# First two stripes side by side on the raw input, a third and layer 1's second one in float32, layer norm's additions on VectorE, two heads kept in SBUF

## The chip, the cores and the metric

The kernel runs on one core of one Trainium2 chip. A core has a matrix engine (TensorE, PE in the profile), a vector engine (VectorE, DVE), an activation engine (ScalarE, ACT), a general engine (GpSimd, POOL) and queues that start DMA transfers (SP is SyncE, whose only work here is to start them). The engines run their own instruction lists in order and wait for each other by semaphores. The metric is the device time of one execution in microseconds (us), the median over runs.

## The reference

Two residual layers over 528 rows (16 meta tokens and 512 inputs) of width 2048, and a final norm. Cut to what matters:

```python
def even_mixer(hn, ...):                       # layer 0
    glu_v, glu_g, gate_a, q, c, gate_b, qi, ki, wi = split_last(hn @ w_in, EVEN_SPLITS)
    u = causal_depthwise_conv(glu_v * sigmoid(glu_g), width=31) + conv_b
    a_out = silu(layer_norm(u, ln_g, ln_b)) * silu(gate_a)
    c = rms_norm(c, kv_g)                      # 256 columns, the shared keys and values
    ...                                        # index scores from qi, ki, wi pick 128 keys a query
    b_out = (attention of 8 heads over the picked keys) * silu(gate_b)
    return concatenate([a_out, b_out]) @ w_out
def odd_mixer(hn, ...):                        # layer 1
    q, fz, i, g = split_last(hn @ w_in, 4 x 2048)
    ...                                        # gated linear recurrence, 16 heads, chunks of 64
    return (rms_norm per head of the recurrence * silu(g)) @ w_out
for layer in range(2):
    h = h + mixer(rms_norm(h, norm_gain[layer]))
return rms_norm(h, final_norm_gain)[:, 16:]
```

## The kernel before, in words

Everything is kept transposed: 128 features on the partitions, the 528 rows (T) along the free axis, usually as two halves of 264 (HT). A width of 2048 is 16 tiles (KT). The weights arrive as stripes: w[s] is 128 x 2048 in float32, 1 MB, all that is needed for 128 outputs. `load_raw` brings one into a ring of three buffers (`w32`; `w` in the profile).

There are two ways to multiply a stripe. `stripe` works on a normalised input that has been split into two float16 parts (X0 in layer 0, X1 in layer 1; tiles `x` and `mx`). ACT sums the stripe's squares (L192, `junk`), POOL adds them over the partitions (`all_sum`, L144, an all-reduce), VectorE makes a power-of-two scale of it (L148 to L201), ACT and VectorE split the weights into `wh` (L208) and `wl` (L209), in two halves each and rings of five; then PE does three float16 products for each of the 16 tiles and each column half, 96 matmuls (L251 to L253). A stripe with `wide=False` leaves the meta rows out and has 48 matmuls of 512 columns. `raw_stripe` works on the input as it is, in float32: VectorE multiplies the norm's gain into the weights (L264), PE does one float32 product for each tile and half (L267; the trace shows two passes for each), and the evacuation multiplies by the row's reciprocal norm (`evac`, L279). It needs neither X nor rstd to begin.

At the start, 16 x tiles (names z, Kh, Vt, mb, from the rings that are free then) and the first weights come through SP's queue in the order of the code. ACT squares each x tile (L377, L380), VectorE adds the squares in three groups (L381), PE sums them over the partitions with a matrix of ones (`mean_bcast`, L304, `ones_d`), ACT makes rstd0 of it by a logarithm and an exponential (`rstd_from`, L311 and L312), and VectorE and ACT make X0 from it (L388, then `split`: L293 on ACT, L294 on VectorE). kw (80 columns: index keys and index weights) is a raw stripe on these tiles; its evacuation is followed by four small transposes on PE (L409). The two stripes of c are c0, a raw stripe, and c1, an ordinary one.

Then come eight gated convolutions (`glu`), 64 scores and selections, the layer norm and eight heads, in a hand-written order of steps. `layer_norm` sums the eight convolved tiles Z, takes the mean from Z[i] (L675) and sums the squares: ACT squares (L680), POOL adds (L681, tile `acc`), and PE takes the mean square (L304 with `ones_a`). Each head leaves its output tile `mb` in DRAM (`mbd`, L647). Before the output projection all eight are read back (L732), scaled by a factor that depends on all of layer 0's statistics and split into `mx` (the last one into an `x`).

Layer 1 begins with fz of head 0, a raw stripe on the residual sum h, then the mean and rstd1, X1 (L793 and `split`), and q and v of head 0 as ordinary stripes. For each of 16 heads three stripes (fz, q, v) go through PE, and `rec_head` does the recurrence of that head beside them. On POOL's queue `send` prepares sums of later weights in DRAM, one or two steps after each ordinary stripe.

The program order on each engine is set by a scheduler that simulates the program when it is built and takes, among ready instructions, those of the highest priority band: WGT (weights, X), EVAC (evacuations, norms), SIDE (attention, gates, recurrence), CONV (convolution, layer norm). `queued[...]` and `behind(...)` (`issue_after`) hold an instruction back until another one has been placed. So a change of one part can move instructions elsewhere.

Of the kernel before, what the change touches and what calls it, by code (L numbers as in the profile page):

```python
# [74 lines left out]
def trunk_kernel(ctx: ExitStack, tc: tile.TileContext, x: bass.AP, w: bass.AP, wukv: bass.AP,  # L75
# [5 lines left out]
    def band(level):  # L81
        return tc.high_priority(level * 1000000)
# [149 lines left out]
    def columns(wide):  # L232
        return (slice(0, HT), slice(HT, T)) if wide else (slice(NM, T),)
# [19 lines left out]
                    P.matmul(o, lo[half][:, ws], xh[:, sl], start=False, stop=n == 1 and k == 7)  # L253
        return parts, inv

    def raw_stripe(w32, X, gain, m=128, ring=None):

        ring = [r or bank for r in ring or (None, None)]
        parts = [(r(), sl) for r, sl in zip(ring, columns(True))]
        parts = [(p[:, :sl.stop - sl.start], sl) for p, sl in parts]  # L260
        with band(WGT):
            for n in range(2):
                v = w32[:, 1024 * n:1024 * (n + 1)].rearrange("p (k m) -> p k m", m=128)[:, :, :m]
                V.tensor_tensor(v, v, vec[:, gain + 8 * n:gain + 8 * n + 8, None].to_broadcast([128, 8, m]), op=OP.mult)  # L264
        for k in range(KT):
            for o, sl in parts:
                P.matmul(o[:m], w32[:, k * 128:k * 128 + m], X[k][:, sl], start=k == 0, stop=k == KT - 1)  # L267
        return parts

    def put(dst, parts, inv):  # L270

# [4 lines left out]
    def evac(dst, parts, rstd):  # L276
        o = T - dst.shape[-1]
        for p, sl in parts:
            V.tensor_tensor(dst[:, sl.start - o:sl.stop - o], p[:dst.shape[0]], rstd[:dst.shape[0], sl],  # L279
                            op=OP.mult)  # L280
# [27 lines left out]
    def rstd_from(pieces, dst, eps, tmp=None):  # L308

        for p, sl in pieces:  # L310
            S.activation(dst[:, sl], p, AF.Ln, bias=eps)  # L311
            S.activation(dst[:, sl], dst[:, sl], AF.Exp, scale=-0.5)  # L312
            if tmp is not None:
                t = tmp[:, sl]
                S.activation(t, dst[:, sl], AF.Square)
                V.scalar_tensor_tensor(t, p, eps, t, op0=OP.add, op1=OP.mult)
                S.activation(t, t, AF.Identity, scale=-0.5, bias=c15)
                V.tensor_tensor(dst[:, sl], dst[:, sl], t, op=OP.mult)


    bdram = dram.tile([HB, 16, BL], F32, name="bdram")
# [33 lines left out]

    X0 = []
    xin = []
    with band(WGT + 1):
        for k in range(KT):
            shape, name, bufs = STAGE[k]  # L360
            hin = et(shape, F32, name, bufs)
            if len(shape) > 2:
                hin = hin.rearrange("p a b -> p (a b)")
            hin = hin[:, :T]
            Q.dma_start(hin, x[k])
            if k == 0:
                wkw = load_raw(S_KW, 2)
            if k == 11:
                wc = load_raw(S_C)
            xin.append(hin)  # L370
    sums = []
    with band(EVAC):
# [8 lines left out]
                V.tensor_tensor(acc0, acc0, sq, op=OP.add)  # L381
    rstd0 = et([128, T], F32, "rstd", 1)
    with band(EVAC):
        rstd_from(mean_bcast(ones_d, sums, None, ring=(pso, ps1)), rstd0, eps_r)
    with band(WGT):
        for k in range(KT):
            t = et([128, T], F32, "sq", 3)
# [11 lines left out]


    kw = et([128, T], F32, "qh", 2)
    ps = raw_stripe(wkw, xin, V_G0, m=80)
    with band(EVAC):
        evac(kw[:80], ps, rstd0)
    wiT = et([128, NB, NM], F32, "wiT", 1)
    with band(SIDE):
        p = ps1()
        for t in range(NB):
            P.transpose(p[:, t * NM:(t + 1) * NM], kw[64:80, NM + 128 * t:NM + 128 * (t + 1)],  # L409
                        ident[64:80, 64:80])  # L410
        V.tensor_scalar(wiT.rearrange("p a b -> p (a b)"), p[:, :NB * NM], 1.0 / 32, None, op0=OP.mult)

        ki = et([128, T], F32, "gt", 3)
        G.dma_start(ki[:64], kw[:64])
        G.dma_start(ki[64:], kw[:64])


        kih = epools["ei"].tile([128, T], F32R, name="kih", bufs=1)
        kil = epools["ei"].tile([128, T], F32R, name="kil", bufs=1)
        S.activation(kih, ki, AF.Identity)  # L420
        V.tensor_tensor(kil[:64], ki[:64], kih[:64].bitcast(F32), op=OP.subtract)
        V.tensor_tensor(kil[64:], ki[64:], ki[64:], op=OP.subtract)
# [6 lines left out]
    csq = []  # L429
    for j in range(2):  # L430
        c = et([128, T], F32, "gb", 2)
        if j == 0:
            ps = raw_stripe(wc, xin, V_G0, ring=(ps1, ps1))
            with band(EVAC):
                evac(c, ps, rstd0)
        else:
            ps, inv = stripe(S_C + j, X0, back0, ring=(None, ps1))
            with band(EVAC):
                put(c, ps, inv)
        with band(SIDE):  # L440
            sq = et([128, T], F32, "sq", 3)
            S.activation(sq, c, AF.Square)
        cn.append(c)
        csq.append(sq)
# [152 lines left out]
    def attend(h, qh, gb, Kh, Vt):  # L597
# [46 lines left out]
        p = ps1()  # L644
        P.matmul(p[:, :NM], Vt[:NM, 0, :], pt[:NM, 0, :NM], start=True, stop=True)
        V.tensor_tensor(mb[:, :NM], p[:, :NM], gb[:, :NM], op=OP.mult)
        Q.dma_start(mbd[h], mb)  # L647

    def head(h):
        if h % 2 == 0:  # L650
# [13 lines left out]
    def layer_norm():  # L664
        with band(CONV):
            zs = et([128, T], F32, "acc", 2)
            V.tensor_tensor(zs, Z[0], Z[1], op=OP.add)
            for i in range(2, 8):
                V.tensor_tensor(zs, zs, Z[i], op=OP.add)
            mu = et([128, T], F32, "acc", 2)  # L670
            for p, sl in mean_bcast(ones_a, [zs], None):
                S.activation(mu[:, sl], p, AF.Copy)
            vs_ = et([128, T], F32, "acc", 2)
            for i in range(8):
                V.tensor_tensor(Z[i], Z[i], mu, op=OP.subtract)  # L675
                if i == 0:
                    S.activation(vs_, Z[i], AF.Square)
                else:
                    sq = et([128, T], F32, "sq", 3)
                    S.activation(sq, Z[i], AF.Square)  # L680
                    G.tensor_tensor(vs_, vs_, sq, op=OP.add)  # L681
            rz = et([128, T], F32, "acc", 2)
            rstd_from(mean_bcast(ones_a, [vs_], None), rz, eps_l)
        return rz
# [26 lines left out]
    with band(SIDE):  # L711
# [13 lines left out]
        V.tensor_scalar(c[6], mscale, 0.25, None, op0=OP.mult)  # L725
        V.tensor_scalar(c[7], mscale, 0.5, None, op0=OP.mult)
        for i in range(8):
            shape, name = (([128, T], "Kh"), ([128, 5, 128], "Vt"), ([128, T], "L"))[i // 3]
            mb = et(shape, F32, name, 3)
            if len(shape) > 2:  # L730
                mb = mb.rearrange("p a b -> p (a b)")[:, :T]
            Q.dma_start(mb, mbd[i])  # L732
            MX[8 + i] = split(r1p.tile([128, 2, T], F16, name="mx" if i < 7 else "x", bufs=7 if i < 7 else KT), mb, c[7])
        for i in range(8):
            MX[i] = split(r1p.tile([128, 2, T], F16, name="x", bufs=KT), MA[i], c[6])
# [44 lines left out]
                V.tensor_tensor(acc1, acc1, sq, op=OP.add)  # L780
            S.dma_start(h1d[n], hin)
    with band(WGT):
        wfz = load_raw(S_FQV)
    ps0 = raw_stripe(wfz, H1, V_G1)
    with band(EVAC):
        with tc.issue_after(done.ins):
            S.preload_act_table_set("natural_log_exp_and_others")
# [198 lines left out]
    for h in range(16):  # L986
# [2 lines left out]
        v = ht([128, T], F32, "v", 2)  # L989
        if h == 0:  # L990
            with band(EVAC):
                evac(fz, ps0, rstd1)
        for dst, i in ((fz, 0), (q, 1), (v, 2)):
            if h or i:
                ps, inv = stripe(S_FQV + 3 * h + i, X1, back1, wide=i != 1)
                with band(EVAC):
                    put(dst, ps, inv)
                send(todo, 1 + i % 2)
# [328 lines left out]
```

## Time and profile before

| | before |
|---|---|
| median of 3 runs | 1872.37 us (1872.37, 1875.14, 1872.37) |
| the profiled execution | 1873.82 us, span 1872.0 us, mean granted PE clock 0.986 |
| PE busy | 1815.4 us, 97% |
| VectorE busy | 1339.1 us, 72% |
| ACT busy | 1203.5 us, 64% |
| POOL busy | 194.7 us, 10% |
| DMA | 272.79 MB, mean 146 GB/s |

A timeline row reads: start in us, busy us of the group, engine, line, operation, output tile <- input tiles, shape, and xN for the number of instructions in the group; in brackets the idle time of that engine just before, and what ended it. A row of waits reads: who waited, the tile and line it waited to work on, <- whose result on which tile and line; then us in total, how often, and the longest. A windows row gives, after the stretch and its length, the busy time of PE, PE's weight loads, DVE, ACT and POOL, then the granted PE clock, the share of the DMA engines that was busy, and GB/s. Lines are those of the kernel before.

### The profile page before, as it was taken

How to read it: one execution, taken by the hardware profiler on the slowest of the kernel's cores; microseconds unless marked ns; L12 is line 12 of the kernel's file. 1: busy time of each engine (PE TensorE's matmuls, PEld its weight loads, DVE VectorE, ACT ScalarE, POOL GpSimd, SP SyncE). 2: the span in 40 equal slices, each digit the busy share in tenths (PEclk: the TensorE clock that was granted, in tenths of full speed). 3: DMA queues.
4: the chain of work that ended last, by engine and by line, in shares of the span. 5: the costliest groups of instructions: out<-in, count | busy, mean ns of one | idle time of the engine just before them, and what ended most of it. 6: DMA issues, size and time to landing. Idle time of an engine off the chain costs nothing.

```text
span 1872.0 us, 36780 instructions
## 1 busy us (share of the span) xinstructions
PE 1815.4 (97%) x14934; PEld 1405.2 (75%) x14934; DVE 1339.1 (72%) x2758; ACT 1203.5 (64%) x1941; POOL 194.7 (10%) x353
## 2 busy tenths in 40 slices
PE   8999999899999599999999999999999999999997
PEld 5777578788888577888677777777777775446886
DVE  7699999997565255444586777777777776666775
ACT  6655665466555565444578887788877877765562
POOL 1100100121211222000111001010110000001000
PEclk9999999999999799999999999999999999999999
DMA  6432333234344145333465554554545345656553
GB/s 246 112 102 96 96 112 103 83 114 126 104 140 127 37 132 182 136 122 137 143 182 161 168 169 140 177 170 159 169 142 152 122 151 179 207 197 229 202 190 112
DMA packets 65434, 272.79 MB, mean 146 GB/s; under 512 B 8272, under 2 KB 15736, under 8 KB 48144
## 3 DMA queue, kind: packets, MB, share of 16 engines
q1 hardware_dynamic: 36128, 180.36, 27.1%
q0 software_dynamic: 17616, 52.19, 11.7%
q10 hardware_dynamic: 11520, 37.88, 6.0%
q8 instruction: 117, 1.92, 0.4%
q14 instruction: 53, 0.43, 0.1%
HBM read 251.30 MB, written 40.58 MB: 156 GB/s over the span
## 4 chain that ended last, share of the span: by engine, by line
PE 89%; DVE 4%; DMA 3%; ACT 2%; issue 2%; POOL 1%; SPq 0%; DVEq 0%; POOLq 0%; ACTq 0%
PE mps L252 23%; PE mps L251 23%; PE mps L253 23%; PE mps L1145 8%; PE po L635 1%; PE s L610 1%; DVE mask L556 1%; PE s L267 1%; DVE m L555 1%; PE s L846 1%; PE s L845 1%; PE s L847 1%; PE po L968 1%; PE po L967 1%; DMA w<-in_w_dram 1%
## 5 line engine op out<-in xcount | busy, mean ns | idle before, releaser
L251 PE MATMUL mps<-x,wh 128*128 128x264 f16 (+1 forms) x3216 | 955.8, 297 | 5.4 <-ACT x L293 2.2
L252 PE MATMUL mps<-x,wh 128*128 128x264 f16 (+1 forms) x3216 | 956.0, 297 | 1.7 <-DVE x L294 1.7
L253 PE MATMUL mps<-x,wl 128*128 128x264 f16 (+1 forms) x3216 | 955.7, 297 | 0.0
L252 PEld LDWEIGHTS <-wh 128*128 128x128 f16 x3456 | 339.0, 98 | 128.0 <-issue 16.2
L253 PEld LDWEIGHTS <-wl 128*128 128x128 f16 x3456 | 339.0, 98 | 117.2 <-issue 5.5
L251 PEld LDWEIGHTS <-wh 128*128 128x128 f16 x3456 | 338.9, 98 | 116.8 <-issue 4.1
L208 ACT ACTIVATE wh<-w,sc 128x1024 f16<-128x1024 f32 x224 | 256.0, 1145 | 260.3 <-PE mps L252 225.1
L209 DVE SCALAR_TENSOR_TENSOR wl<-w,sc,wh 128x1024 f16<-128x1024 f32 x224 | 287.4, 1284 | 141.3 <-ACT wh L208 140.8
L192 ACT ACTIVATE junk<-w 128x2048 bf16<-128x2048 f32 (+1 forms) x116 | 214.7, 1851 | 3.7 <-DMA w<-in_w_dram 3.1
L581 DVE SCALAR_TENSOR_TENSOR z<-u,vec,z 128x528 f32<-128x528 f32 x240 | 181.0, 761 | 2.3
L144 POOL PARTITION_ALL_REDUCE tot<-ss x96 | 43.6, 454 | 893.2 <-ACT junk L192 827.2
L1145 PEld LDWEIGHTS <-wh 128*128 128x128 f16 x912 | 89.2, 98 | 10.9 <-issue 0.3
L208 ACT ACTIVATE wh<-w,oq 128x1024 f16<-128x1024 f32 x53 | 60.7, 1148 | 54.6 <-PE mps L1145 46.3
L209 DVE SCALAR_TENSOR_TENSOR wl<-w,oq,wh 128x1024 f16<-128x1024 f32 x53 | 67.8, 1283 | 27.9 <-ACT wh L208 27.7
L1145 PE MATMUL mps<-on,wh 128*128 128x256 f16 x464 | 78.1, 273 | 0.1
L192 ACT ACTIVATE junk<-gw 128x1024 bf16<-128x1024 f32 x64 | 67.3, 1052 | 2.1 <-DMA gw<-in_w_dram 0.8
L251 PE MATMUL mps<-mx,wh 128*128 128x264 f16 x224 | 62.3, 278 | 3.8 <-ACT gt L274 3.8
L842 DVE SCALAR_TENSOR_TENSOR qlm<-q,qhm 128x256 f16<-128x256 f32 x128 | 52.5, 420 | 17.0 <-ACT qhm L841 16.9
L1145 PE MATMUL mps<-on,wl 128*128 128x256 f16 x232 | 63.2, 273 | 0.0
L841 ACT ACTIVATE qhm<-q 128x256 f16<-128x256 f32 x128 | 51.4, 415 | 18.4 <-DVE q L943 18.3
L253 PE MATMUL mps<-mx,wl 128*128 128x264 f16 x224 | 62.4, 279 | 0.0
L252 PE MATMUL mps<-mx,wh 128*128 128x264 f16 x224 | 62.4, 279 | 0.0
(437 smaller groups left out, 2844.1 us busy)
## 6 DMA issues: line engine op xcount, KB each, us to landing
w<-in_w_dram SPq DMA_DIRECT2D x132, 1024.0 KB, 4.9
gw<-in_w_dram ACTq DMA_DIRECT2D x64, 512.0 KB, 7.0
os<-in_w_dram POOLq DMA_DIRECT2D x42, 512.0 KB, 8.3
w<-os SPq DMA_DIRECT2D x28, 512.0 KB, 4.4
w<-in_w_dram SPq DMA_DIRECT2D x23, 512.0 KB, 4.6
os<-os POOLq DMA_DIRECT2D x14, 512.0 KB, 6.1
h<-in_x_dram POOLq DMA_DIRECT2D x16, 264.0 KB, 6.7
h1d<-h ACTq DMA_DIRECT2D x16, 264.0 KB, 2.2
```

The lines of the kernel that those rows point to most:

```text
L144: queued["G"] = G.partition_all_reduce(out, src, channels=128, reduce_op=op or bass_isa.ReduceOp.add)
L192: S.activation(junk[:, :src.shape[-1]], src, AF.Square, accum_out=ss)
L208: queued["S"] = S.activation(hi, src, AF.Identity, scale=sc)
L209: V.scalar_tensor_tensor(lo, src, sc, hi, op0=OP.mult, op1=OP.subtract)
L251: P.matmul(o, hi[half][:, ws], xh[:, sl], start=n == 0 and k == 0, stop=False)
L252: P.matmul(o, hi[half][:, ws], xl[:, sl], start=False, stop=False)
L253: P.matmul(o, lo[half][:, ws], xh[:, sl], start=False, stop=n == 1 and k == 7)
L267: P.matmul(o[:m], w32[:, k * 128:k * 128 + m], X[k][:, sl], start=k == 0, stop=k == KT - 1)
L581: eng.scalar_tensor_tensor(z, u[:, j:j + T], col(V_CW + i * CW + j), z, op0=OP.mult, op1=OP.add)
L841: S.activation(hi, src, AF.Copy, scale=scale)
L842: V.scalar_tensor_tensor(lo, src, scale, hi, op0=OP.mult, op1=OP.subtract)
L1145: P.matmul(p, wt[:, sl], xt, start=start and k == i == 0, stop=stop and k == 7 and i == 2, skip_group_check=stop and not start and resume)
```

## The change

Five edits:

- `raw_stripes` takes the place of `raw_stripe`: it takes several stripes and goes through the 16 tiles once, doing each tile for all of them. kw and c0 go through it together; c1 follows as a raw stripe of its own. c0's weight is loaded behind the fourth x tile (it was the twelfth), c1's behind the eleventh.
- The four transposes behind kw are held back until the last raw matmul of these has been placed, and the weights' square sums until rstd0's last instruction.
- The layer norm's seven additions of squares go from POOL to VectorE.
- Heads 6 and 7 of layer 0 keep their tile `mb` in SBUF; six heads go through DRAM. The six are read into the rings Kh and Vt in turn, and L is not used.
- In layer 1 v of head 0 is a raw stripe behind fz, with its weight loaded beside fz's. It has no `send` of its own.

```diff
-    def raw_stripe(w32, X, gain, m=128, ring=None):
+    def raw_stripes(X, gain, todo):
...
+        jobs = []
+        for w32, m, ring in todo:
...
         for k in range(KT):
-            for o, sl in parts:
-                P.matmul(o[:m], w32[:, k * 128:k * 128 + m], X[k][:, sl], start=k == 0, stop=k == KT - 1)
-        return parts
+            for w32, m, parts in jobs:
+                for o, sl in parts:
+                    queued["P"] = P.matmul(o[:m], w32[:, k * 128:k * 128 + m], X[k][:, sl],
+                                           start=k == 0, stop=k == KT - 1)
+        return [parts for w32, m, parts in jobs]
...
-            if k == 11:
-                wc = load_raw(S_C)
+            if k in (3, 10):
+                wc.append(load_raw(S_C + k // 10))
...
-        rstd_from(mean_bcast(ones_d, sums, None, ring=(pso, ps1)), rstd0, eps_r)
+        queued["S"] = rstd_from(mean_bcast(ones_d, sums, None, ring=(pso, ps1)), rstd0, eps_r)
...
-    ps = raw_stripe(wkw, xin, V_G0, m=80)
+    ps, cps = raw_stripes(xin, V_G0, [(wkw, 80, (None, None)), (wc[0], 128, (ps1, ps1))])
+    cps = [cps] + raw_stripes(xin, V_G0, [(wc[1], 128, (None, ps1))])
...
-        for t in range(NB):
+        with behind("P"):
+          for t in range(NB):
             P.transpose(p[:, t * NM:(t + 1) * NM], kw[64:80, NM + 128 * t:NM + 128 * (t + 1)],
...
-        if j == 0:
-            ps = raw_stripe(wc, xin, V_G0, ring=(ps1, ps1))
-            with band(EVAC):
-                evac(c, ps, rstd0)
-        else:
-            ps, inv = stripe(S_C + j, X0, back0, ring=(None, ps1))
-            with band(EVAC):
-                put(c, ps, inv)
+        with band(EVAC):
+            evac(c, cps[j], rstd0)
...
-        Q.dma_start(mbd[h], mb)
+        if h < 6:
+            Q.dma_start(mbd[h], mb)
+        else:
+            MB.append(mb)
...
-                    G.tensor_tensor(vs_, vs_, sq, op=OP.add)
+                    V.tensor_tensor(vs_, vs_, sq, op=OP.add)
...
-            shape, name = (([128, T], "Kh"), ([128, 5, 128], "Vt"), ([128, T], "L"))[i // 3]
-            mb = et(shape, F32, name, 3)
+            shape, name = (([128, T], "Kh"), ([128, 5, 128], "Vt"))[i % 2]
+            mb = MB[i - 6] if i >= 6 else et(shape, F32, name, 3)
...
-            Q.dma_start(mb, mbd[i])
+            if i < 6:
+                Q.dma_start(mb, mbd[i])
...
-        wfz = load_raw(S_FQV)
-    ps0 = raw_stripe(wfz, H1, V_G1)
+        wfz, wv = load_raw(S_FQV), load_raw(S_FQV + 2)
+    ps0 = raw_stripes(H1, V_G1, [(wfz, 128, (None, None))])
+    ps0 += raw_stripes(H1, V_G1, [(wv, 128, (ps1, ps1))])
...
-                evac(fz, ps0, rstd1)
+                evac(fz, ps0[0], rstd1)
+                evac(v, ps0[1], rstd1)
         for dst, i in ((fz, 0), (q, 1), (v, 2)):
-            if h or i:
+            if h or i == 1:
```

What it moves, in the order of the instructions. Lines of the kernel after are a few higher: L267 is L271 there, L304 is L309, L602 and L604 are L605 and L607. First PE at the start: the x tiles are z (the first eight), Kh, Vt and mb; `w_203` is kw's weight in both, `w_228` before and `w_212` after that of c0; `po` and `s_288` (`s_290` after) are the two halves of the mean. Before:

```order
L267 MATMUL mps<-z,w_203 80x264 x14
L304 MATMUL po<-acc,ones_d 128x264
L304 MATMUL s_288<-acc,ones_d 128x264
L267 MATMUL mps<-z,w_203 80x264 x2
L267 MATMUL mps<-Kh,w_203 80x264 x5
L304 MATMUL po<-acc,ones_d 128x264
L304 MATMUL s_288<-acc,ones_d 128x264
L267 MATMUL mps<-Kh,w_203 80x264
L267 MATMUL mps<-Vt,w_203 80x264 x6
L267 MATMUL mps<-mb,w_203 80x264 x4
L304 MATMUL po<-L,ones_d 128x264
L304 MATMUL s_288<-L,ones_d 128x264
```

After, around the last pair of ones:

```order
L271 MATMUL mps<-Kh,w_203 80x264 x2
L271 MATMUL s_383<-Kh,w_212 128x264
L271 MATMUL s_384<-Kh,w_212 128x264
L309 MATMUL po<-L,ones_d 128x264
L309 MATMUL s_290<-L,ones_d 128x264
L271 MATMUL mps<-Kh,w_203 80x264 x2
L271 MATMUL s_383<-Kh,w_212 128x264
L271 MATMUL s_384<-Kh,w_212 128x264
L271 MATMUL mps<-Vt,w_203 80x264 x2
L271 MATMUL s_383<-Vt,w_212 128x264
L271 MATMUL s_384<-Vt,w_212 128x264
```

Before, the last pair of ones stands behind all 32 matmuls of kw; now behind 20 of kw and 20 of c0, with nine tiles of kw ahead of c0's first row and the two stripes in turn from the tenth tile on.

POOL around the layer norm; `stat<-ss` is an all-reduce of a stripe's squares, a row of `ISA` without tiles stands where POOL turns to another kind of operation, the DMAs are those of the heads' bias rows. Before:

```order
L144 ISA stat<-ss 128x1
L681 ISA
L681 TENSOR_TENSOR acc<-acc,sq 128x528 x6
L144 ISA
L144 ISA stat<-ss 128x1
L681 ISA
L681 TENSOR_TENSOR acc<-acc,sq 128x528
L144 ISA
L144 ISA stat<-ss 128x1
```

After:

```order
L605 DMA L<-bdram 128x1x400
L607 DMA L<-mask_580 128x400
L144 ISA stat<-ss 128x1 x3
L605 DMA L<-bdram 128x1x528
L607 DMA L<-mask_583 128x528
L144 ISA stat<-ss 128x1
```

The seven additions have left, and the turns with them.

PE at the start of layer 1; the tiles h are the residual sums, `w_10655` is fz's weight before, `w_10568` after, `w_10570` that of v, and the rows with `ones_d` are the mean. Before:

```order
L267 MATMUL mps<-h_9262,w_10655 128x264 x2
L267 MATMUL mps<-h_9389,w_10655 128x264
L304 MATMUL s_10694<-acc_8621,ones_d 128x264
L304 MATMUL s_10696<-acc_8621,ones_d 128x264
L267 MATMUL mps<-h_9389,w_10655 128x264
L267 MATMUL mps<-h_9516,w_10655 128x264 x2
```

After:

```order
L271 MATMUL mps<-h_10191,w_10568 128x264 x2
L271 MATMUL s_10608<-h_8538,w_10570 128x264
L271 MATMUL s_10609<-h_8538,w_10570 128x264
L309 MATMUL s_10645<-acc_8534,ones_d 128x264
L309 MATMUL s_10647<-acc_8534,ones_d 128x264
L271 MATMUL s_10608<-h_8540,w_10570 128x264
L271 MATMUL s_10609<-h_8540,w_10570 128x264
```

The mean stood behind 17 of fz's 32 matmuls; it stands behind all 32 and the first pair of v, and 15 pairs of v follow it ahead of q.

More of the change, by code (lines that the diff above doesn't have):

```diff
@@ L254, in stripe @@
         return parts, inv
-    def raw_stripe(w32, X, gain, m=128, ring=None):
[L258 to L264, printed above, removed]
-        for k in range(KT):
-            for o, sl in parts:
-                P.matmul(o[:m], w32[:, k * 128:k * 128 + m], X[k][:, sl], start=k == 0, stop=k == KT - 1)
-        return parts
+    def raw_stripes(X, gain, todo):
+        jobs = []
+        for w32, m, ring in todo:
+            ring = [r or bank for r in ring]
+            parts = [(r(), sl) for r, sl in zip(ring, columns(True))]
+            jobs.append((w32, m, [(p[:, :sl.stop - sl.start], sl) for p, sl in parts]))
+            with band(WGT):
+                for n in range(2):
+                    v = w32[:, 1024 * n:1024 * (n + 1)].rearrange("p (k m) -> p k m", m=128)[:, :, :m]
+                    V.tensor_tensor(v, v, vec[:, gain + 8 * n:gain + 8 * n + 8, None].to_broadcast([128, 8, m]),
+                                    op=OP.mult)
+        for k in range(KT):
+            for w32, m, parts in jobs:
[3 more added lines that the diff above has]
+        return [parts for w32, m, parts in jobs]
     def put(dst, parts, inv):
@@ L311, in rstd_from @@
             S.activation(dst[:, sl], p, AF.Ln, bias=eps)
-            S.activation(dst[:, sl], dst[:, sl], AF.Exp, scale=-0.5)
+            done = S.activation(dst[:, sl], dst[:, sl], AF.Exp, scale=-0.5)
             if tmp is not None:
@@ L318, in rstd_from @@
                 V.tensor_tensor(dst[:, sl], dst[:, sl], t, op=OP.mult)
+        return done
     bdram = dram.tile([HB, 16, BL], F32, name="bdram")
@@ L357, in trunk_kernel @@
     xin = []
+    wc = []
     with band(WGT + 1):
@@ L727, in trunk_kernel @@
         for i in range(8):
-            shape, name = (([128, T], "Kh"), ([128, 5, 128], "Vt"), ([128, T], "L"))[i // 3]
-            mb = et(shape, F32, name, 3)
-            if len(shape) > 2:
+            shape, name = (([128, T], "Kh"), ([128, 5, 128], "Vt"))[i % 2]
+            mb = MB[i - 6] if i >= 6 else et(shape, F32, name, 3)
+            if len(mb.shape) > 2:
                 mb = mb.rearrange("p a b -> p (a b)")[:, :T]
-            Q.dma_start(mb, mbd[i])
+            if i < 6:
+                Q.dma_start(mb, mbd[i])
             MX[8 + i] = split(r1p.tile([128, 2, T], F16, name="mx" if i < 7 else "x", bufs=7 if i < 7 else KT), mb, c[7])
```

## Prediction

> **What bounds the kernel now.** I read the page's first table and its chain first, then PE's waits over the whole span, then the timelines of PE, ACT, DVE, POOL and SP around the four places that the change touches.
>
> ```profile
> span 1872.0 us, 36780 instructions
> PE 1815.4 (97%) x14934; PEld 1405.2 (75%) x14934; DVE 1339.1 (72%) x2758; ACT 1203.5 (64%) x1941; POOL 194.7 (10%) x353
> PE 89%; DVE 4%; DMA 3%; ACT 2%; issue 2%; POOL 1%; SPq 0%; DVEq 0%; POOLq 0%; ACTq 0%
> ```
>
> PE is busy 1815.4 of 1872.0 us and carries 89% of the chain that ended last. So time can leave in two ways only: PE waits less (56.6 us in all), or PE has less to do, which includes running less at half clock. The list of PE's waits says where those 56.6 us lie:
>
> ```profile
> PE s L304 <- POOL acc L681: 20.0, 1, 20.0
> PE s L409 <- DVE qh L279: 5.2, 1, 5.2
> PE mps L251 <- ACT gt L274: 5.1, 3, 3.8
> ```
>
> In order: the layer norm's mean square, the wait before the four small transposes at the start, and the start of layer 0's output projection. The change touches these three and a fourth place, layer 1's first stripes, where the waits are short and many (part 4). I price one after the other.
>
> **1. Layer norm: seven additions go from POOL to VectorE.**
>
> ```profile
> 609.49 9.07 POOL L681 TENSOR_TENSOR acc<-acc,sq 128x528 f32<-128x528 f32 x6 [9.99 <-issue]
> 626.13 0.40 POOL L144 PARTITION_ALL_REDUCE stat<-ss  x1 [7.57 <-issue]
> 633.71 1.28 POOL L681 TENSOR_TENSOR acc<-acc,sq 128x528 f32<-128x528 f32 x1 [7.18 <-issue]
> 600.54 5.03 DVE L675 TENSOR_TENSOR z<-z,acc 128x528 f32<-128x528 f32 x8
> 605.49 1.27 DVE L209 SCALAR_TENSOR_TENSOR wl<-w,sc,wh 128x1024 f16<-128x1024 f32 x1
> 602.46 1.15 ACT L208 ACTIVATE wh<-w,sc 128x1024 f16<-128x1024 f32 x1
> 610.82 0.64 ACT L680 ACTIVATE sq<-z 128x528 f32<-128x528 f32 x1 [5.78 <-POOL acc L681]
> 615.18 1.90 ACT L192 ACTIVATE junk<-w 128x2048 bf16<-128x2048 f32 x1
> 635.05 2.13 PE L304 MATMUL s<-acc,ones_a 128*128 128x264 f32 x4 [20.04 <-POOL acc L681]
> 619.00:638.00 19.00, 2.95 (x9) 2.54 (x10) 1.71 (x4) 3.68 (x5) 1.69 (x2) 0.50 0.16 64
> ```
>
> POOL stands 9.99, 7.57 and 7.18 us ("issue": nothing that the trace shows) each time it turns from a reduction to an addition or back, and an addition there takes 1.3 us or more. The seventh addition lies behind both turns, so PE stands 20.04 us, until 635.05. With the additions on VectorE the three reductions follow each other without a turn. VectorE's addition: 5.03/8 = 0.63 us. It has 8 subtractions (5.03), one L209 (1.27) and 7 additions (4.4) from 600.54 on, so it could be done at 611.2. ACT sets the pace: its row order stays, with one weight split and the 1.90 us junk square ahead of the last square. The split before stood at 602.46; they come when PE frees a buffer, some 6 to 7 us apart there, so this one at 609.3; the junk ends at 612.3 with its 0.2 us read, the square at 612.9, the last addition at 613.6. PE's arrival was 635.05 - 20.04 = 615.0, and it now has a few more matmuls first. So the wait goes entirely, with 1.4 us to spare. Behind the idleness PE ran at half clock: the last row (a stretch, then PE's busy time, and after POOL's the granted clock) has 2.95 busy us at 0.50, of which half, 1.5, is lost. Term: 20.0 + 1.5 = 21.5. Next to come late is the split for the stripe behind; its all-reduce no longer waits 7.57 us, so I take nothing. Bounds: 22 above; below 11.5, if ACT's and VectorE's chain comes a stripe's length (10 us) late.
>
> **2. Heads 6 and 7 kept in SBUF.**
>
> ```profile
> 721.94 0.33 SPq L732 DMA_DIRECT2D L<-mbd  x1
> 728.14 0.74 ACT L293 ACTIVATE x<-L,mxb 128x528 f16<-128x528 f32 x1 [7.54 <-DMA L<-mbd]
> 736.09 0.46 ACT L274 ACTIVATE gt<-mps,inv 128x264 f32<-128x264 f32 x1
> 738.00:741.00 3.00, 3.00 (x16) 2.03 (x15) 2.00 (x3) 0.86 (x2) 0.00 (x0) 0.50 0.40 167
> ```
>
> ACT stood 7.54 us for head 7's tile to return from DRAM. Everything behind on ACT moved with it, up to the evacuation at 736.09 that gave PE its bank: PE waited 3.8 us (the longest of the three in the list) and then ran 3.00 us at half clock, 1.5 lost. Without the loads ACT comes up to 7.5 us sooner, more than the 3.8 that PE waited. Term 3.8 + 1.5 = 5.3; bounds 3 (ACT then waits for another operand) and 6. SP loses two stores and two loads, and nothing queues there.
>
> **3. The start: kw and c0 advance together, c1 also in float32.**
>
> ```profile
> 9.36 6.50 PE L267 MATMUL mps<-z,w 128*80 128x264 f32 x28
> 31.77 0.28 PE L409 MATMUL s<-ident,qh 16*128 16x16 f32 x1 [5.22 <-DVE qh L279]
> 31.98 9.02 PE L267 MATMUL s<-z,w 128*128 128x264 f32 x26
> 49.77 0.28 PE L251 MATMUL mps<-x,wh 128*128 128x264 f16 x1
> 916.03 6.84 PE L267 MATMUL mps<-h,w 128*128 128x264 f32 x30
> 32.00:33.00 1.00, 1.00 (x3) 0.82 (x3) 1.00 (x3) 1.00 (x3) 0.12 (x1) 0.50 0.44 115
> 30.17 0.72 ACT L312 ACTIVATE rstd<-rstd 128x264 f32<-128x264 f32 x2
> 10.28 3.49 ACT L380 ACTIVATE sq<-z 128x528 f32<-128x528 f32 x5 [4.24 <-DMA z<-in_x_dram]
> 10.00:12.50 2.50, 2.50 (x12) 1.55 (x11) 1.81 (x3) 1.98 (x4) 0.00 (x0) 1.00 1.05 396
> 59.63 0.72 ACT L293 ACTIVATE x<-sq,gains 128x528 f16<-128x528 f32 x1
> ```
>
> From layer 1's raw stripe (the row at 916.03; the next stripe begins at 922.71, part 4) a pass of 264 float32 columns takes 6.68/30 = 0.2227 us, so a raw stripe of 64 passes 14.25. An f16 stripe of 96 matmuls takes 10.80 (v in part 4, 940.85 to 951.65). Before, f16 work begins at 49.77, and c1's share of it ends the part that the change replaces at 49.77 + 10.80 = 60.57. After, PE does three raw stripes (192 passes) and 12 passes of ones: 204 x 0.2227 = 45.4. From 9.36 that ends at 54.8 if PE never stands.
>
> It does stand: at 396 to 400 GB/s a 1 MB weight takes 2.6 us and an x tile 0.69. c0's weight now goes behind the fourth x tile instead of the twelfth, so the fifth tile lands 2.6 later: ACT begins on the second at 10.28, so the fifth was there at 10.28 + 3 x 0.69 = 12.35, and is now at 14.95. PE has done four k's of kw by then (each 4 passes, 0.89) at 12.95. So 2.0 us of idleness, and 0.4 for the transposes: 57.2. Term 60.57 - 57.2 = 3.4. c1's 14.25 against 10.8 is in it. What hides the rest: the gain folds of c0 and c1 on VectorE fall between the x additions, before PE asks for either stripe, and a fold that comes late makes PE wait for it; the evacuations move beside the f16 stripe.
>
> Who is late next: the mean (last ones at about 31 instead of 25.9), and with it rstd0, which gains table loads on ACT too, and X0. X0's last split stood within two or three us of 60 with rstd0 ready at 30.17 + 0.72 = 30.9; some 6 us later it is 66, and the first f16 stripe asks for its sixteenth tile at 57.2 + 15 x 0.675 = 67.3 (six matmuls of 0.1125 a tile). That is tight. Bounds: above 5.4, if PE doesn't stand at 12.95; below -2, if X0 comes some 5 us late.
>
> Whether the 2.0 us of idleness halve the clock decides 1.5 more. Before, the clock fell behind 3.8 us (part 2) and behind 5.22 (0.50 in the row at 32 us). It also fell behind the 2.24 of part 4, though shorter pieces of idleness stood ahead of that one. I take no fall, since 2.0 stands alone and below all three; with it the term would be 1.9. The Trainium skill ("TensorE: Matmul & The Clock Gate", Part 1, the table of states) has the clock fall after one idle window of about 3.4 us. By that the term stays 3.4 here; but the 2.24 us of part 4 was followed by half clock, which that rule alone doesn't give.
>
> **4. Layer 1: the first v stripe in float32, after fz.**
>
> ```profile
> 915.79 0.93 ACT L311 ACTIVATE rstd<-s,eps_r 128x264 f32<-128x264 f32 x2 [5.14 <-PE s L304]
> 917.37 1.95 DVE L793 TENSOR_TENSOR sq<-h,rstd 128x528 f32<-128x528 f32 x3 [6.62 <-ACT rstd L312]
> 922.71 0.38 PE L251 MATMUL mps<-x,wh 128*128 128x512 f16 x1
> 926.59 0.38 PE L251 MATMUL mps<-x,wh 128*128 128x512 f16 x1
> 932.64 0.58 PE L251 MATMUL mps<-x,wh 128*128 128x512 f16 x1 [2.24 <-ACT x L293]
> 934.00:936.00 2.00, 2.00 (x6) 0.69 (x5) 2.00 (x4) 0.73 (x1) 2.00 (x3) 0.50 0.98 383
> 938.72 1.65 DVE L294 SCALAR_TENSOR_TENSOR x<-sq,gains,x 128x528 f16<-128x528 f32 x2
> 940.85 0.27 PE L251 MATMUL mps<-x,wh 128*128 128x264 f16 x1
> 951.65 0.28 PE L251 MATMUL mps<-x,wh 128*128 128x264 f16 x1
> 952.00:1492.00 540.00, 540.00 (x5154) 418.97 (x5152) 418.51 (x1000) 429.35 (x721) 50.27 (x103) 1.00 0.51 158
> ```
>
> The q stripe (48 matmuls; the first 18 took 926.59 - 922.71 = 3.88, so 10.35 in all) ran from 922.71 to 940.85: 18.14 us, 7.8 lost to X1 coming tile by tile and to the half clock that followed. v then ended at 951.65. After, raw v occupies PE from 922.7 to 936.9, and q could end at 947.3: a gain of 4.4 at most. But the order puts the mean behind all of fz and one pair of v: it ends at 922.7 + 0.9 = 923.6, where it was 916.0 (the next fz passes began at 916.03). VectorE started 1.3 us behind the mean and took from 917.37 to 938.72 + 1.6, 22.9 us, for X1. So now 924.9 to 947.8; q's last matmuls follow, 948.6. Term 951.65 - 948.6 = 3.1; bounds 4.4 and -2, if rstd1 comes 5 us later still behind the weight work that ACT now does first.
>
> In the 15 heads behind, the order shifts the recurrence about one stripe later. I cost that at nothing: PE stood nowhere from 952 to 1492 (540.00 of 540.00), while DVE and ACT were busy 78% and 80%, so each has a fifth of a stripe's time, 2 us, to catch up in.
>
> **The sum**: 21.5 + 5.3 + 3.4 + 3.1 = 33.3 us. The profiled execution took 1873.8 with its span of 1872.0, so 1840.5 against it; it stands 1.45 above the median of 1872.37, against which I predict 1839.1. All terms at their upper ends give 37.8 (1834.6), all at the lower 10.5 (1861.9). What this measurement can tell from no change is 0.2%, 3.7 us.
>
> **The rivals.**
>
> Late layer norm (0.10). The last square on ACT stands behind the weight split at 609, which waits for PE to free a buffer, and that is the only cover: if it slips a stripe, 10 us of wait and the cold clock return. Term 11.5 instead of 21.5, so 1849. Against it: VectorE and ACT both had several us without work there (5.78 on ACT's row at 610.82, for POOL alone).
>
> Nothing from the two ends (0.16). X0 and X1 come late, and PE's waits only move: terms 3 and 4 are -2 each instead of 6.5 together, so 1849.6. For it: both rest on a mean that comes 5 to 7 us later than before, and X0's margin is about one us. Against it: the raw stripes are work that needs neither, 14.25 us each.
>
> Slower (0.05): the shifted recurrence costs PE in each of layer 1's later heads. PE runs in order, so if a head's transposes stand at its front while ACT or DVE is late with their operands, the whole next stripe waits behind them. At 2.2 us a head (15 x 2.2 = 33) the gain is gone; at 3 us the kernel is 45 - 33.3 = 11.7 slower than before, 1884. For it: ACT at 80% and DVE at 78% have little to spare. Against it: the old order held the same work without one wait, and a shift by a whole stripe gives operands more time, not less.
>
> The change doesn't do what it says (0.03, 1872): something else turns POOL between its kinds of work, so that PE waits as long for a reduction as it did for the additions. Against it: POOL's new order shows nothing but reductions and DMAs there.
>
> **How the numbers follow.** My forecast, 1839.1 with its own range of 1833 to 1845 (waits of up to 6 us more or less in terms 3 and 4), has 0.66. The late layer norm and the two ends, 0.26 together, take the range to 1854, 5 us above their own times; above that lie the last two rivals and both mishaps at once, some 0.13. I go to 1831 below, which leaves 0.04. Faster by over 0.2%: 0.66 + 0.10 + 0.16 = 0.92. Same: 0.03. Slower: 0.05.
>
> **What would show it.** Right: PE's waits without the 20.0 on acc, and POOL's reductions between 600 and 640 without gaps of 7 us before them; no DMA ahead of ACT's x near 728; PE idle about 2 us near 13 and at full clock behind it; the first f16 stripe of layer 0 begun near 57; layer 1's q without a wait above 1.5 us and ended near 948 less what was gained before. Wrong: PE's waits sum to over 25 us, the clock falls near 15, the mean square still waits for acc, or waits stand in the heads of layer 1.

## The result, and the profile after

The changed kernel takes 1853.19 us (median of 4 runs, 1850.70 to 1855.38) against 1872.37: ratio 0.9896, interval 0.9878 to 0.9913. So 19 us are gained where I forecast 33.3. It lies inside the range by 0.8 us, and in the sum of the prediction 14 us are missing. Its profiled execution took 1855.38 with a span of 1853.6, 18.4 below that of before.

The page's first lines, the rows of PE's waits over the whole span that matter here (PE's gaps of over 0.2 us sum to 21.7 us behind its first instruction, where before had 43.1), and POOL's timeline around the layer norm:

```profile
span 1853.6 us, 36583 instructions
PE 1818.7 (98%) x14870; PEld 1412.4 (76%) x14870; DVE 1337.6 (72%) x2763; ACT 1191.4 (64%) x1937; POOL 183.5 (10%) x344
```

```profile
PE s L631 <- ACT L L622: 9.0, 5, 2.8
PE s L546 <- DMA uh<-ql: 3.1, 1, 3.1
PE s L853 <- ACT qhm L849: 2.3, 2, 2.1
...
PE mps L271 <- DMA z<-in_x_dram: 0.9, 1, 0.9
PE s L509 <- ACT Kh L498: 0.8, 1, 0.8
...
PE mps L252 <- DVE x L299: 0.5, 1, 0.5
```

```profile
605.71 0.60 POOL L144 PARTITION_ALL_REDUCE stat<-ss  x1
617.72 0.39 POOL L144 PARTITION_ALL_REDUCE stat<-ss  x1 [11.41 <-ACT junk L192]
639.79 0.39 POOL L144 PARTITION_ALL_REDUCE stat<-ss  x1 [21.69 <-ACT junk L192]
```

All the waits that the change was aimed at have gone: 20.0 on acc, 5.2 at the transposes, the 3.8 of the output projection, and the row of waits in layer 1's q but for 0.5. POOL waits for ACT's square sums only. But new waits stand there: 3.1 for a DMA of the first scores (L546, in `scores`), 2.3 before the last recurrence (L853), and 9.0 instead of 5.8 in the heads (L631).

Where the time went is seen by counting PE's float16 products in both traces and comparing when the same one begins. c1's 96, which only before has, are not counted there:

| place | before, us | after, us | gained so far |
|---|---|---|---|
| 300th product | 103.4 | 99.2 | 4.2 |
| 400th | 117.5 | 119.3 | -1.9 |
| 1500th, selections | 303.8 | 308.8 | -5.1 |
| 3500th, ahead of layer norm | 595.1 | 601.8 | -6.7 |
| 3700th, behind it | 648.4 | 631.0 | 17.5 |
| 4200th, ahead of the output projection | 726.4 | 713.7 | 12.7 |
| 5700th, late in it | 900.8 | 882.5 | 18.4 |
| fz of head 1 begins | 951.7 | 930.0 | 21.7 |
| v of head 15 ended | 1535.0 | 1510.0 | 25.0 |
| last product of `stripe` | 1708.2 | 1690.0 | 18.2 |

The start's 4.2 us are gained and then lost, with 6.7 more, before the layer norm; layer 1 gains 6.6 until its last head and gives 6.8 back behind it.

The first row overstates what the start is worth, since one trace stands on each side. Near 31 us PE runs at half clock in every trace with the old start, for 6.8 us in before and two others and for 3.4 in four. Over all seven of them the 300th product begins at 101.4 to 103.4, over the seven with the new start at 99.2 to 100.9: the mean lead is 2.4 us.

### The profile page after: what moved, and what is told of

It reads as the page before. It is cut to its first block, busy times and chain, and to the rows that moved or that the text cites. A ratio compares the mean times of both kernels' runs of the same rounds, so it can differ in the third digit from the quotient of the medians.

```text
span 1853.6 us, 36583 instructions
## 1 busy us (share of the span) xinstructions
PE 1818.7 (98%) x14870; PEld 1412.4 (76%) x14870; DVE 1337.6 (72%) x2763; ACT 1191.4 (64%) x1937; POOL 183.5 (10%) x344
## 4 chain that ended last, share of the span: by engine, by line
PE 90%; DVE 5%; ACT 2%; DMA 1%; issue 1%; SPq 0%; POOL 0%; ACTq 0%; DVEq 0%
PE mps L251 22%; PE mps L252 22%; PE mps L253 22%; PE mps L1154 8%; PE mps L271 2%; PE po L638 1%; PE s L271 1%; PE s L613 1%; DVE mask L559 1%; DVE m L558 1%; PE s L854 1%; PE s L853 1%; DVE wl L209 1%; PE s L855 1%; PE po L976 1%; PE po L975 1%
## 5 line engine op out<-in xcount | busy, mean ns | idle before, releaser
L251 PE MATMUL mps<-x,wh 128*128 128x264 f16 (+1 forms) x3168 | 942.2, 297 | 3.2 <-ACT gt L571 1.9
L252 PE MATMUL mps<-x,wh 128*128 128x264 f16 (+1 forms) x3168 | 942.0, 297 | 0.5 <-DVE x L299 0.5
L253 PE MATMUL mps<-x,wl 128*128 128x264 f16 (+1 forms) x3168 | 941.8, 297 | 0.0
L252 PEld LDWEIGHTS <-wh 128*128 128x128 f16 x3392 | 332.7, 98 | 119.0 <-issue 6.4
L253 PEld LDWEIGHTS <-wl 128*128 128x128 f16 x3392 | 332.6, 98 | 115.4 <-issue 2.6
L251 PEld LDWEIGHTS <-wh 128*128 128x128 f16 x3392 | 332.9, 98 | 113.0 <-issue 4.0
L208 ACT ACTIVATE wh<-w,sc 128x1024 f16<-128x1024 f32 x220 | 251.1, 1144 | 198.9 <-PE mps L252 175.8
L209 DVE SCALAR_TENSOR_TENSOR wl<-w,sc,wh 128x1024 f16<-128x1024 f32 x220 | 281.1, 1280 | 104.6 <-ACT wh L208 104.4
L192 ACT ACTIVATE junk<-w 128x2048 bf16<-128x2048 f32 (+1 forms) x114 | 210.9, 1850 | 12.2 <-DMA w<-in_w_dram 8.5
L1154 PEld LDWEIGHTS <-wh 128*128 128x128 f16 x912 | 89.2, 98 | 11.0 <-issue 0.3
L849 ACT ACTIVATE qhm<-q 128x256 f16<-128x256 f32 x128 | 51.0, 411 | 17.5 <-DVE q L951 16.1
```

The source lines that it names most:

```text
L192: S.activation(junk[:, :src.shape[-1]], src, AF.Square, accum_out=ss)
L208: queued["S"] = S.activation(hi, src, AF.Identity, scale=sc)
L209: V.scalar_tensor_tensor(lo, src, sc, hi, op0=OP.mult, op1=OP.subtract)
L251: P.matmul(o, hi[half][:, ws], xh[:, sl], start=n == 0 and k == 0, stop=False)
L252: P.matmul(o, hi[half][:, ws], xl[:, sl], start=False, stop=False)
L849: S.activation(hi, src, AF.Copy, scale=scale)
```

## The experiments

Theory A: the stretch from 94 to 290 us belongs to VectorE, and what PE gains ahead of it cannot get through. Theory B: the start is worth its 4 us, and the losses are luck. Theory C: in layer 1 the raw v saves time at the front, and the recurrence that it pushes back is paid at the end. The page of before had the sign for A: VectorE's digits stand at 9 in the slices from 94 to 420 us. The same window of both kernels (stretch, length, then busy time of PE, its loads, VectorE, ACT, POOL, and the granted clock), before and after:

```profile
94.00:240.00 146.00, 146.00 (x993) 100.23 (x990) 143.39 (x247) 82.32 (x128) 17.55 (x26) 1.00 0.31 101
```

```profile
94.00:240.00 146.00, 142.93 (x955) 98.11 (x953) 142.61 (x243) 80.67 (x124) 16.98 (x25) 0.98 0.31 96
```

VectorE is busy 98% in both, with PE full too before. In after ACT stands 5.28 us for a scale that VectorE makes of a stripe's sums, and the half rows of the first scores (`uh`), for which PE waits near 101, come behind that:

```profile
97.21 1.15 ACT L208 ACTIVATE wh<-w,sc 128x1024 f16<-128x1024 f32 x1 [5.28 <-DVE sc L199]
98.27 0.67 ACT L533 ACTIVATE uh<-mps,inv 64x512 fp32r<-64x512 f32 x1
```

**e1_no_start**: the changed kernel with the old start.

```diff
-            if k in (3, 10):
-                wc.append(load_raw(S_C + k // 10))
+            if k == 11:
+                wc.append(load_raw(S_C))
...
-    ps, cps = raw_stripes(xin, V_G0, [(wkw, 80, (None, None)), (wc[0], 128, (ps1, ps1))])
-    cps = [cps] + raw_stripes(xin, V_G0, [(wc[1], 128, (None, ps1))])
+    ps, = raw_stripes(xin, V_G0, [(wkw, 80, (None, None))])
...                                   # c0 raw and c1 as a stripe, where they stood; no behind("P")
```

> The start as before (c0 behind kw, c1 an ordinary f16 stripe), the other three edits kept. Theory A: the start's 4 us never get through, because VectorE is busy 98% of the stretch from 94 to 240 us and its convolutions begin 1.1 us later with the new start, and PE pays for its lead with new waits; by the aligned traces the new start stands at -6.7 us by 600. Then this kernel takes 1846 to 1849. Theory B: the start is worth its 4 us, and the new waits come from the luck of DMA landings or from the clock: 1856 to 1858.

Measured: 1849.62 us, ratio 0.9874 (0.9861 to 0.9888), 3.6 below the whole change by the medians, with intervals that overlap by a little. It is 0.6 above A's range; B's 1856 to 1858 is out.

**e2_start_only**: only the new start (the start's part of the diff above), the other three edits undone.

> The new start alone on the kernel before. Theory A: 1874 to 1879, slower than before, with PE waiting near 101 us for the half rows of the first scores and the clock falling behind it. Theory B: 1868.

Measured: 1876.77 us, ratio 1.0026 (1.0017 to 1.0035): 5.0 slower than before by the medians, as A had it. PE waits for the same DMA (the whole stretch from 57 to 130 us has this one wait), and the clock, which I expected to fall, stays full from 101 to 108:

```profile
PE s L546 <- DMA uh<-ql: 2.9, 1, 2.9
```

```profile
101.00:108.00 7.00, 4.06 (x34) 3.22 (x32) 6.86 (x11) 5.18 (x9) 1.74 (x3) 1.00 0.35 77
```

**e4_two_logs**: why VectorE's convolutions begin later with the new start. ACT's timeline before, around the norm of c (`rc`):

```profile
72.27 0.83 ACT L311 ACTIVATE acc<-s,eps_r 128x264 f32<-128x264 f32 x2
73.00 0.42 ACT L312 ACTIVATE acc<-acc 128x264 f32<-128x264 f32 x1
73.43 1.28 ACT L568 ACT_TABLE_LOAD   x1
...
75.10 0.41 ACT L312 ACTIVATE acc<-acc 128x264 f32<-128x264 f32 x1
```

and after (with the evacuation of the first convolution's input, L279):

```profile
72.28 1.28 ACT L316 ACT_TABLE_LOAD   x1
73.58 0.48 ACT L316 ACTIVATE acc<-s,eps_r 128x264 f32<-128x264 f32 x1
74.07 1.28 ACT L317 ACT_TABLE_LOAD   x1
75.37 0.42 ACT L317 ACTIVATE acc<-acc 128x264 f32<-128x264 f32 x1
75.81 1.28 ACT L316 ACT_TABLE_LOAD   x1
77.10 0.48 ACT L316 ACTIVATE acc<-s,eps_r 128x264 f32<-128x264 f32 x1
...
77.91 1.28 ACT L317 ACT_TABLE_LOAD   x1
...
88.54 0.46 ACT L279 ACTIVATE gt<-mps,inv 128x264 f32<-128x264 f32 x1
```

The order of ACT now alternates logarithm, exponential, logarithm, exponential behind a tanh, and each switch loads a table: four loads of 1.28 us. Before, both logarithms stood ahead of the tanh, with the tables that the start had left. The first convolution on VectorE starts at 89.53 before and at 90.61 after (at 87.7 in e1, which has the old start).

```diff
-        rstd_from(mean_bcast(ones_c, csq, None), rc, eps_r, et([128, T], F32, "sq", 3))
+        pieces = mean_bcast(ones_c, csq, None)
+        for p, sl in pieces:
+            ln = S.activation(rc[:, sl], p, AF.Ln, bias=eps_r)
+        with tc.issue_after(ln.ins):
+            ...                       # then the exponentials and the correction of each half
```

> The changed kernel with the norm of c written as two logarithms and then two exponentials, so that ACT has two table loads there instead of four (2 x 1.28 = 2.56 us off its queue at 72 to 80). Theory A (what counts is when VectorE's convolutions begin, and ACT's loads hold them): convolutions begin up to 2.5 us earlier, near 88.1, the wait near 101 shrinks below 1 us, the clock stays full, and 3 to 5 us are gained: 1848 to 1850. Theory B: PE sets the pace there, so nothing moves, 1853 within 1.

Measured: 1849.29 us, ratio 0.9875 (0.9861 to 0.9888), 3.9 below the whole change by the medians, in A's range; the two intervals overlap by a little. In its trace the first convolution starts here:

```profile
88.27 0.55 DVE L593 TENSOR_SCALAR z<-u,vec 128x528 f32<-128x528 f32 x1
```

That is 2.3 us sooner. PE waits nowhere from 57 to 279, and the 400th product begins 5 us sooner than in after: the wait of 3.1 at 101 is gone, and the half clock behind it, 6.8 us long and so 3.4 lost. So the extra loads caused that loss: with two of them gone VectorE's convolutions and ACT's `uh` (95.94 instead of 98.27) both come 2.3 us sooner.

**e8_c_norm_later**: e4, and the norm of c issued only behind that evacuation.

```diff
+        if step == EVEN[0]:
+            with behind("E"):         # queued["E"]: the evacuation of the first convolution's input
+                make_cx()
```

> The changed kernel with the norm of c (two logarithms, then two exponentials) held back until the first convolution's input has been evacuated, so that VectorE's convolutions begin before it. Theory A: they begin near 84 to 86 us instead of 90.6, and nearly all of the start's 4 us comes through: 1845 to 1847. Rival: PE's own work, or VectorE having the same work to do later in a stretch in which it is 98% busy, sets the end, and it is no better than with the two logarithms alone: 1849.

Measured: 1851.21 us, ratio 0.9885 (0.9872 to 0.9899): A's 1845 to 1847 is out, and the rival holds. The convolutions begin at 86.0 as expected, but the twentieth tap (of the 30 additions that follow a convolution's first product) starts at 118.5, where e4 had 113.1, since the norm's work now falls among them; PE is 0.2 us from e4 by the 2500th product. Starting VectorE sooner on one thing by putting another behind it gained nothing here, where all of it must be done.

**f1_start_half_taps and f2_no_start_half_taps**: a pair to tell the theories apart. Both leave out 15 of 31 taps of every convolution, so that VectorE has room and the output is another one; f1 has the new start with e4's two logarithms, f2 the old start.

```diff
-            for j in range(1, CW):
+            for j in range(1, 16):
```

> The changed kernel with the two logarithms first (as in e4_two_logs), and with 15 of the 31 taps of every convolution left out (120 of VectorE's additions of 0.76 us, some 91 us of its work; the output is another one). To be held against f2_no_start_half_taps, the same with the old start. Theory A (VectorE's full queue between 94 and 290 us swallows what PE gains before it): with VectorE unloaded the gain comes through, and this kernel is 3 to 4 us faster than f2_no_start_half_taps, where with all taps the two starts stand level (1849.3 and 1849.6). Theory B (the new start's lead is lost for another reason, such as later weights or X0): it stays level or is slower.

> The old start with the other three edits (as e1_no_start), and with 15 of the 31 taps of every convolution left out. Theory A: 3 to 4 us slower than f1_start_half_taps. Theory B: level with it or faster.

Measured: 1842.51 us (ratio 0.9837, 0.9823 to 0.9850) and 1847.11 us (0.9863, 0.9850 to 0.9876): the new start is 4.6 us faster, where with all taps the two are level (1849.29 and 1849.62). VectorE's share of 94 to 240, in f1 and in f2, is 78% and 77%:

```profile
94.00:240.00 146.00, 145.99 (x989) 99.85 (x988) 114.11 (x201) 83.67 (x132) 13.12 (x27) 1.00 0.32 102
```

```profile
94.00:240.00 146.00, 146.00 (x993) 100.25 (x991) 112.75 (x197) 83.05 (x131) 11.93 (x25) 1.00 0.31 101
```

The sign is as theory A forecast it and the size a little above its 3 to 4 us, but the traces do not bear its reason out. The 4.6 us are not all the start's lead: f1 leads f2 by 1.8 us at the 300th product, by 1.6 at the 1000th (at 207 us) and by 4.6 at the 1950th, where f2 has waited 1.5 us more between 294 and 315 and run at half clock for 6.8 us instead of 3.4. And a full VectorE does not stop the lead. With all taps e4 leads e1 by 1.7 us at the 300th product and still by 1.2 at the 1000th, although VectorE is busy for 143.9 of e4's 146 us from 94 to 240; f3 leads f4 (two more kernels with the new and the old start, described below) by 3.5 and 3.2. At the 1500th e4 is 2.2 behind e1, and f3 1.8 behind f4. In between PE waits at 279 and at 296, in e4 for 1.81 and 1.49 us, in e1 at neither. At the first ACT stands for a weight, in e1 and then in e4; at the second VectorE itself stands for a mask in e4:

```profile
277.43 1.91 ACT L192 ACTIVATE junk<-w 128x2048 bf16<-128x2048 f32 x1 [1.74 <-DMA w<-in_w_dram]
```

```profile
278.58 1.91 ACT L192 ACTIVATE junk<-w 128x2048 bf16<-128x2048 f32 x1 [4.14 <-DMA w<-in_w_dram]
293.31 0.31 DVE L626 CUSTOM_DVE_ANT_0 L<-s,L 128x144 f32<-128x144 f32 x1 [1.62 <-DMA L<-mask]
```

That weight takes 4.8 to 5.0 us from issue to landing in all seven traces with the old start, 5.7 to 6.7 in after, e2, e4, e5 and f3, and 4.9 and 4.8 in e8 and f1. The mask takes 2.7 to 2.9 with the old start and all taps, 3.8 to 4.6 in the same five, but also 5.3 in f2. So what is left of the lead dies at transfers that land late, as theory B allowed. Why they are slower there, and whether VectorE's load has a part in it, these runs do not show.

**e3_ln_only**: the layer norm's line alone, on the kernel before.

```diff
-                    G.tensor_tensor(vs_, vs_, sq, op=OP.add)
+                    V.tensor_tensor(vs_, vs_, sq, op=OP.add)
```

> Layer norm's additions on VectorE, alone on the kernel before. If the term was sized rightly: 20.0 of wait and 1.9 of half clock go, 1850.5. If ACT and VectorE pay for it in the heads behind, where PE's idleness had given them a lead (after shows 4.7 us of waits and 10 us at half clock near 660 to 673, before 3.0 and 6.8 near 677), 3 to 4 us come back: 1853.5 to 1854.5.

Measured: 1854.61 us, ratio 0.9901 (0.9887 to 0.9914), 17.2 gained by the medians, 16.1 to 21.2 by the interval. By counted products 24.2 are gained at the layer norm by the 3700th, and 19.5 of them are left from the 3900th on. So the second of the two expectations holds (its range ended 0.1 lower): some of the gain is paid back in the heads behind. PE's waits in before from 600 to 690, then in after from 600 to 680, and after's clock behind them:

```profile
PE s L304 <- POOL acc L681: 20.0, 1, 20.0
PE s L628 <- ACT L L619: 2.2, 1, 2.2
PE s L645 <- DVE pt L643: 0.7, 1, 0.7
```

```profile
PE s L631 <- ACT L L622: 3.3, 2, 2.0
PE s L648 <- DVE pt L646: 0.7, 1, 0.7
PE po L638 <- ACT pt L636: 0.6, 1, 0.6
```

```profile
663.00:673.00 10.00, 7.26 (x30) 5.70 (x30) 6.21 (x16) 6.27 (x17) 2.91 (x4) 0.50 0.59 146
```

After has 1.7 us more of waiting there and 10.2 us at half clock where before had 6.8; e3's own trace has the same waits and the same 10.2.

**e6_mx_only**: only the two heads kept in SBUF.

```diff
-        Q.dma_start(mbd[h], mb)
+        if h < 6:
+            Q.dma_start(mbd[h], mb)
+        else:
+            MB.append(mb)
...                                   # and the reading back, as in the change
```

> Heads 6 and 7 kept in SBUF, alone on the kernel before: the wait of 3.8 us at the output projection's start and 1.5 to 1.7 at half clock behind it go, 1866.5. If the tiles come late in another way, 1868 to 1870.

Measured: 1868.76 us, ratio 0.9981 (0.9972 to 0.9991): 4.5 us gained by the medians, 1.7 to 5.2 by the interval. The time lies in the range of the other expectation, 1868 to 1870, but only because the kernel before ran at 1873.30 in this comparison: PE's wait at the output projection is gone. In its trace the place itself gains 5.4, as the term had it: the two traces are level at the 1950th product and 5.4 apart at the 4400th.

**e5_no_l1, e7_l1_only, f3_two_logs_no_l1, f4_ln_mx**: layer 1's raw v taken from the changed kernel, put alone on the one before, taken from e4, and taken together with the new start.

```diff
-        wfz, wv = load_raw(S_FQV), load_raw(S_FQV + 2)
+        wfz = load_raw(S_FQV)
...
-    ps0 += raw_stripes(H1, V_G1, [(wv, 128, (ps1, ps1))])
...                                   # and v as an ordinary stripe behind q
```

> The changed kernel with layer 1 begun as before (only fz raw). If the raw v is worth the 3.1 us of the prediction's term, 1856.3. Theory C: the q stripe's waits go, but the raw v takes 3.4 us more and the recurrence, moved one stripe later, is left over at the end of the heads, where PE waits 2.3 us near 1545; net worth zero: 1852.5 to 1853.5.

> The raw v of layer 1 alone on the kernel before. By the prediction's term 1868.7. By theory C 1871 to 1873, with PE's q stripe without waits above 1 us and a new wait of about 2 us before the last head's products.

> The new start with the two logarithms first, layer norm on VectorE and the heads in SBUF, but layer 1 begun as before. If the raw v is worth nothing, level with e4_two_logs, 1849 to 1851; if it was worth 3, 1852 to 1853.

> Only layer norm's additions and the two heads, on the kernel before. If start and raw v together cost what the single runs say (4 and 0 us), 1849 to 1850, 3 to 4 below the whole change; if layer 1's raw v is worth 3 here, 1852.5.

Measured: e5 1855.03 (0.9903, 0.9889 to 0.9917), e7 1874.96 (1.0008, 0.9999 to 1.0017), f3 1849.49 (0.9872, 0.9858 to 0.9885), f4 1849.09 (0.9872, 0.9859 to 0.9886). With and without the raw v: 1853.19 and 1855.03, 1849.29 and 1849.49, 1849.62 and 1849.09 (e1 and f4), and alone between level and 3.2 us slower than before, where the term said 3.1 faster. e5 lies between its two forecasts, e7 2 us above theory C's, f3 and f4 where a raw v worth nothing puts them. By the times it is worth nothing that these runs can tell, as theory C has it. Layer 1 of after on PE, raw stripes first, the q stripe's one wait, the first matmul of head 1's fz, and the two waits of the last head:

```profile
889.21 14.40 PE L271 MATMUL mps<-h,w 128*128 128x264 f32 x64
903.45 1.05 PE L271 MATMUL s<-h,w 128*128 128x264 f32 x4
904.34 1.05 PE L309 MATMUL s<-acc,ones_d 128*128 128x264 f32 x4
905.23 13.51 PE L271 MATMUL s<-h,w 128*128 128x264 f32 x60
```

```profile
928.75 0.38 PE L252 MATMUL mps<-x,wh 128*128 128x512 f16 x1 [0.53 <-DVE x L299]
...
929.98 0.28 PE L251 MATMUL mps<-x,wh 128*128 128x264 f16 x1
```

```profile
1547.85 0.19 PE L853 MATMUL s<-qhm,kt1h 128*128 128x64 f16 x1 [0.22 <-ACT qhm L849]
1551.72 0.19 PE L853 MATMUL s<-qhm,kt0h 128*128 128x64 f16 x1 [2.09 <-ACT qhm L849]
```

From fz of head 0 to fz of head 1 PE takes 40.8 us, before 44.1. From there to the end of head 15's v 580.1 against 583.4: that 3.3 is not saved, but recurrence work not yet done. From there to the last f16 product of `stripe` 179.9 against 173.1: the left-over work and the 2.3 us of waiting come due. The three stretches add up to 800.7 us in after and 800.6 before. All 14 traces agree: with the raw v (seven) the first takes 40.8 and the last 179.9 to 181.6, without it 44.1 (e6 45.2) and 173.1. This shows theory C more sharply than the times do.

No version tried that keeps all 31 taps beats f4, e4, e1 and f3, which stand level at 1849.1 to 1849.6, about 4 us below the changed kernel.

## Why the prediction was right, and where it was wrong

That the time lies inside the range at all is luck. Two of the four terms, the start and the raw v, gave nothing or cost something, and the range reached to 1854 only to cover mishaps (a late layer norm, a late X0 or X1) that did not happen.

**The layer norm** (21.5): the mechanism and the place are as told. POOL's turns and the wait are gone, and the place gains 24.2. The chain's times hold too: the last addition was to end at 613.6, and ends at 620.5 in a trace that is 6.7 late there.

```profile
619.03 1.52 DVE L687 TENSOR_TENSOR acc<-acc,sq 128x528 f32<-128x528 f32 x2
```

But the term was mis-sized for the whole: 19.5 are left in e3's trace and 17.2 by the medians, whose interval ends at 21.2. I looked behind it only at the next weight split ("I take nothing"). In the heads behind it PE waits 1.7 us more, most of it for the softmax, and runs at half clock for 3.4 us longer. That the 20 us of idleness had let the attention's softmax run ahead fits this, but no run tests it.

**Heads 6 and 7** (5.3): right at its place, 5.4. Alone it is worth 4.5, with 5.2 at the interval's end, so the term was a little high if anything.

**The start** (3.4): the arithmetic of PE came out, partly by offsetting errors. The first f16 stripe begins at 57.02, against 57.2 forecast; the wait for the fifth x tile is 0.87 instead of 2.0, so the rest took about 1 us longer than the sum had it; the clock stays full behind the wait. The base was high: 49.77 in before stands behind 6.8 us at half clock, where four of the seven traces with the old start have 3.4, so the mean lead is 2.4. The step that failed is "Who is late next". I looked at X0, which was in time. I did not ask what VectorE does afterwards, though its row of digits stood on the page, and I put the new table loads at rstd0, where there are none; they came at the norm of c, four of them. VectorE began late, and PE paid 3.1 us of wait and 3.4 of half clock at 101 to 110, as e4 shows. Later waits at 284 and 300 cost 3.1 more, and half clock near 352 1.7. These waits follow transfers that landed late, and why they did is not settled; the half clock near 352 is luck (see the last section).

**Layer 1** (3.1): 3.3 until fz of head 1. The step that failed is "I cost that at nothing": the shifted recurrence costs nothing head by head, as I said and as the rival "slower" denied, but the last head has no stripe behind it to hide under. The mean's late place did less harm than feared: q waited 0.5 us. The prediction put q's lost 7.8 us down to X1 and the half clock together. The half clock cost little or nothing there: from fz of head 0 to fz of head 1 the kernels without the raw v take 44.1 us with none of it (e3), with 3.4 us (e2, e5, f3, f4) and with 6.8 (before); only e6, with 6.8, takes 45.2.

Of the rivals none came as told. "Nothing from the two ends" had the time nearest (1849.6, with the late layer norm's 1849 beside it) and the sign of the start's term, through other mechanisms than a late X0 or X1.

By the medians of the single runs the sum becomes: layer norm 17.2 and heads 4.5 gained, the start 5.0 and the raw v 1.7 lost, together 15.0, where the whole change gains 19.2. They don't add up exactly: each edit also moves the rest, and each run is uncertain by two or three us.

## What to carry to other kernels

Ask of a gain not only whether the bounding engine has less to do there, but who must be in time for it next, the other engines and the transfers: a lead that ends in a wait is lost, and the wait can cost the clock as well. Work that is pushed later is a debt and not a saving until the end of the loop has been priced. And an idle gap can be time in which other engines get ahead: before closing it, look at what they do in it.

## What the runs showed of the hardware

The clock's fall was not a matter of the wait's length alone. Nine traces have a single wait of 2.77 to 2.79 us near 345; half clock followed in after, e1, e3, e4, e5, e6 and e7 and not in before and f4. A wait of 2.94 us at 101 left the clock full in e2; 2.79 at the same place halved it in e5, and 3.07 in after. Half clock also followed 1.94 us near 298 in e2 and 2.08 near 294 in f3. Between the first stripes and the end of layer 1's heads the stretches at half clock lasted 3.4, 6.8, 10.2 or 20.5 us, multiples of 3.4. The Trainium skill ("TensorE: Matmul & The Clock Gate", Part 1) describes a free-running window of 3413 ns and one idle window as the condition; the lengths agree, the falls after 2.8 us show that less than a full window of idleness can suffice. e3 and f4 have the same instructions up to 345 and differ in it, so it is luck, and a wait of 3 us costs 3 to 6.5 us here.

Two logarithms and two exponentials cost two table loads or four by their order alone, 1.28 us each on ACT.
